# A loop that may run no times, put inside a conditional branch (one-core decoder trunk with a mixture of experts)

## The chip, the cores and the metric

The kernel runs on one core of a Trainium2 chip, as one launch. The metric is the device time in microseconds (us) of that launch. A measurement of a kernel is the median over several runs; beside it one execution is taken by the hardware profiler, and all rows below come from that one.

## The reference, cut to what matters

A decoder trunk of two layers on 512 tokens of width 1024. Each layer has a mixer (layer 0: a recurrent head group beside a gating group; layer 1: latent attention), a cross attention into 256 memory tokens, and a mixture of experts. The last is what matters here. Each token goes to the best of 4 groups and there to the best 2 of 8 experts, so 1024 assignments are spread over 32 experts:

```python
h = jax.nn.silu(xb @ w_gate[e]) * (xb @ w_up[e])      # 1024 -> 512
y = h @ w_down[e]                                     # 512 -> 1024
x <- LayerNorm(alpha * x + sum over the token's two experts of gate * y)
```

How many tokens an expert gets is known only at run time. The reference has room for any number.

## The kernel before, in words

**The expert stage** (`moe`, L1843) runs once per layer. It takes the 32 experts two at a time: 16 pairs, each with one tile of 128 rows, 64 for either expert (`CAP = 64`, two column groups of 64 on TensorE). Each pair is an `ExpertRows` object. `gather` (L1683) is an indirect DMA that GpSimd issues: it fetches the pair's 128 rows of h from DRAM into the one tile xg. `turn` (L1693, L1694) transposes them on TensorE (px) and copies them to xT on VectorE. `first` (L1704) does the gate projection into pg, or the up projection into pu, 32 matmuls of 128x512 each. `turn_hidden` (L1716, L1719) transposes the hidden rows hh by 4 matmuls (ph) and copies them back. `second` (L1730) is the down projection into py, 32 matmuls; ScalarE and VectorE split it into a high and a low part (L1736, L1737). `scatter` (L1677) builds a selection matrix on VectorE, and `combine` (L1744, L1754) adds the pair's rows to h by matmuls (pc) and VectorE adds.

**The weights** (`ExpertWeights`, L1494) come in pieces of 1 MB, 12 to a pair: 4 of the gate (wg), 4 of the up (wu), 4 of the down projection (wd). SyncE issues them in the order of use into a ring of buffers, as buffers come free (the `dma_start` is in the helper at L104). The last two pieces of a layer are issued as four halves (L1524). Before the loop below, `load_until_spare` issues what the ring can take, so that one buffer of the ring is left over for the loop; the four halves are asked for behind the loop.

**The extra blocks** (`overflow`, L1757). If an expert has more than 64 tokens, the rest is done in extra blocks of 128 rows. The function counts the blocks on VectorE (`nt`), loads the count into a register of every engine (`values_load`, L1793), and runs a loop of that many turns (`tc.For_i`, L1794). A turn finds its expert, fetches that expert's weights by indirect DMAs into the spare buffer, and does the whole row of gather to combine. The loop's bookkeeping (branches, semaphore events) has the line L1794.

**The order.** `overflow` is called in the turn of the second to last pair (`n == len(X) - 2`), after its gate and up projection and after all of the pair before has been combined. Behind it stand the gather for the last pair, the second to last pair's `turn_hidden`, `second` and `scatter`, and the last pair's `turn`. Then the last pair runs gate, up, combine of the pair before, down, and the layer norm follows. SyncE's and TensorE's order is the program's (`manual_schedule`); that of VectorE, ScalarE and GpSimd is set by the framework's planner, but nothing is moved across the loop. In layer 0 the key projection of the next layer's cross attention (`filler`: memory rows xr, weights wr, splits at L218 and L219, matmuls at L212) runs beside the layer norm.

Of the kernel before, what the change touches and what calls it, by code (L numbers as in the profile page):

```python
# [10 lines left out]
F32 = mybir.dt.float32  # L11
F32R = mybir.dt.float32r
BF16 = mybir.dt.bfloat16
I32 = mybir.dt.int32
AF = mybir.ActivationFunctionType
ALU = mybir.AluOpType
AX = mybir.AxisListType
# [3 lines left out]
P = 128  # L21
T = 512
NT = T // P
D = 1024
KD = D // P
NE = 32
FF = 512
FD = FF // P
# [1728 lines left out]
def overflow(k, pool, work, l, rt):  # L1757

    nc, tc, A, c = k.nc, k.tc, k.A, k.cst
    V = nc.vector  # L1760
    cap = CAP
    NB = 16

    def tl(shape, name, dt=F32):
        return pool.tile([P] + list(shape), dt, name="o" + name)

    cnt = rt["R"][:, NT]
    nb = tl([NE], "nb")
    V.tensor_scalar(nb, cnt, float(cap), None, op0=ALU.is_gt)
    for q in range(1, 4):  # L1770
        V.scalar_tensor_tensor(nb, cnt, float(cap + q * P), nb, op0=ALU.is_gt, op1=ALU.add)
    inc = tl([NE], "inc")
    V.tensor_tensor_scan(inc, c["one"][:, :NE], nb, 0.0, op0=ALU.mult, op1=ALU.add)
    base = tl([NE], "base")
    V.tensor_tensor(base, inc, nb, op=ALU.subtract)
    nt = tl([1], "nt", I32)
    V.tensor_copy(nt, inc[:, NE - 1:NE])

    R = rt["R"][:, :NT]
    t = tl([NT, NE], "t")  # L1780
    V.tensor_scalar(t, R, float(cap), -1.0e6, op0=ALU.is_lt, op1=ALU.mult)
    V.scalar_tensor_tensor(t, R, -float(cap), t, op0=ALU.add, op1=ALU.add)
    b128 = tl([NE], "b128")
    V.tensor_scalar(b128, base, 128.0, None, op0=ALU.mult)
    V.tensor_tensor(t, t, b128[:, None, :].to_broadcast([P, NT, NE]), op=ALU.add)
    key = tl([2, NT], "key")
    tm = tl([NT, NE], "tm")
    for j in range(2):
        V.tensor_tensor(tm, rt["o32"][j], t, op=ALU.mult)
        V.tensor_reduce(key[:, j], tm, axis=AX.X, op=ALU.add)  # L1790
    cur = tl([1], "cur")
    V.tensor_scalar(cur, base[:, 0:1], 0.0, None, op0=ALU.mult)
    n = nc.values_load(nt[0:1, 0:1], min_val=0, max_val=NB - 1)  # L1793
    with tc.For_i(0, n, 1):  # L1794
        c128 = tl([1], "c128")
        V.tensor_scalar(c128, cur, 128.0, None, op0=ALU.mult)
        koff = tl([2, NT], "koff")
        V.tensor_scalar(koff, key, c128, None, op0=ALU.subtract)

        le = tl([NE], "le")  # L1800
        V.tensor_scalar(le, inc, cur, None, op0=ALU.is_le)
        ex = tl([1], "ex")
        V.tensor_reduce(ex, le, axis=AX.X, op=ALU.add)
        V.tensor_scalar(ex, ex, float(l * NE), None, op0=ALU.add)
        wi = tl([2, KD], "wi")
        V.scalar_tensor_tensor(wi[:, 0], ex.to_broadcast([P, KD]), float(D), c["krow"], op0=ALU.mult, op1=ALU.add)
        V.scalar_tensor_tensor(wi[:, 1, :FD], ex.to_broadcast([P, FD]), float(FF), c["frow"], op0=ALU.mult, op1=ALU.add)
        V.tensor_copy(wi[:, 1, FD:], wi[:, 1, :KD - FD])
        wx = tl([2, KD], "wx", I32)
        V.tensor_copy(wx, wi)  # L1810

        po = k.psum("t", name="povt")
        m = 0
        for j in range(2):
            for i in range(NT):
                oh = pool.tile([P, P], F32, name="ooh", tag="ooh", bufs=2)
                V.tensor_scalar(oh, c["iota"], koff[:, j, i:i + 1], None, op0=ALU.is_equal)
                nc.tensor.matmul(po[:, :2], oh, rt["vals"][j][:, i, :], start=(m == 0), stop=(m == 7))
                m += 1
        tg = tl([2], "tg")  # L1820
        V.tensor_copy(tg, po[:, :2])
        ti = tl([1], "ti", I32)
        V.tensor_copy(ti, po[:, 0:1])

        def wts(j, what, half):
            nk, nf = (2, D) if what == "d" else (4, FF)
            v = k.same_tile("wo").rearrange("p (a b) -> p a b", a=nk)
            src = A[{"g": "moe_w_gate", "u": "moe_w_up", "d": "moe_w_down"}[what]]
            for kk in range(nk):
                col = half * nk + kk  # L1830
                nc.gpsimd.indirect_dma_start(
                    out=v[:, kk, :], out_offset=None, in_=src.rearrange("l e r f -> (l e r) f"),
                    in_offset=IndirectOffsetOnAxis(ap=wx[:, 1 if what == "d" else 0, col:col + 1], axis=0))
            return v

        x = ExpertRows(k, pool, work, lambda: tg, lambda: ti, wts, 1)

        x.hidden = lambda: x.xg[:, :FF]
        x.scatter(), x.gather(), x.turn(), x.first("g"), x.first("u"), x.turn_hidden(), x.second(), x.combine()
        V.tensor_scalar(cur, cur, 1.0, None, op0=ALU.add)  # L1840


def moe(k, rs, l, last, filler=None):  # L1843
# [3 lines left out]
    with ExitStack() as st:  # L1847
# [22 lines left out]
        with tc.manual_schedule(engines={mybir.EngineType.PE}):  # L1870
            for n, x in enumerate(X):
                more = n + 1 < len(X)
                x.first("g")
                x.first("u")

                if n:
                    X[n - 1].combine(0, "ccyy")
                if n == len(X) - 2:

                    X[n - 1].combine(2, "cccc")  # L1880
                    W.load_until_spare()
                    overflow(k, pool, work, l, rt)
                    X[n + 1].gather()
                    x.turn_hidden(), x.second(), x.scatter(), X[n + 1].turn()
                    continue
                x.turn_hidden()
                if n:
                    X[n - 1].combine(2, "cccc")
                if more:
                    X[n + 1].turn()  # L1890
                    if n + 3 < len(X):
                        X[n + 2].gather()
                    x.second()
                    x.scatter()
# [189 lines left out]
```

## Time and profile before

| | |
|---|---|
| median of the runs | 2052.22 us (2052.0 to 2052.83, 3 runs) |
| the profiled execution, its own time | 2047.49 us |
| its span, first to last instruction | 2045.7 us |
| mean granted TensorE clock | 0.945 |
| TensorE matmuls busy | 1795.2 us (88%) |
| VectorE, ScalarE, GpSimd busy | 959.0, 449.2, 273.9 us |
| moved by DMA | 522.41 MB |

How to read it: a busy time counts an engine's instructions, not its branches, semaphore events or the issuing of a DMA. The engines' sequencers have rows of their own, with a q behind the name (SPq is SyncE's); branches and events stand there. The expert stages are at about 560 to 1070 us (layer 0) and 1510 to 2046 us (layer 1).

### The profile page before, as it was taken

How to read it: one execution, taken by the hardware profiler on the slowest of the kernel's cores; microseconds unless marked ns; L12 is line 12 of the kernel's file. 1: busy time of each engine (PE TensorE's matmuls, PEld its weight loads, DVE VectorE, ACT ScalarE, POOL GpSimd, SP SyncE). 2: the span in 40 equal slices, each digit the busy share in tenths (PEclk: the TensorE clock that was granted, in tenths of full speed). 3: DMA queues.
4: the chain of work that ended last, by engine and by line, in shares of the span. 5: the costliest groups of instructions: out<-in, count | busy, mean ns of one | idle time of the engine just before them, and what ended most of it. 6: DMA issues, size and time to landing. Idle time of an engine off the chain costs nothing.

```text
span 2045.7 us, 23508 instructions
## 1 busy us (share of the span) xinstructions
PE 1795.2 (88%) x9206; PEld 1104.3 (54%) x9206; DVE 959.0 (47%) x2053; ACT 449.2 (22%) x834; POOL 273.9 (13%) x226
## 2 busy tenths in 40 slices
PE   8778989999789999898497999989969999988945
PEld 6567867878633444343136866778843444333312
DVE  5596466844723333233135666484552333233215
ACT  6314223343200000000022555343220000000000
POOL 3521532400200000000031000130010000000001
PEclk9887989999889999999798999999979999999968
DMA  5111106365789999999954200352869999999961
GB/s 189 54 62 43 31 21 218 122 207 182 301 347 420 421 419 420 421 421 421 400 175 166 83 21 21 103 176 72 340 243 418 421 421 421 420 420 421 421 270 62
DMA packets 124339, 522.41 MB, mean 255 GB/s; under 512 B 11937, under 2 KB 45889, under 8 KB 75585
## 3 DMA queue, kind: packets, MB, share of 16 engines
q1 hardware_dynamic: 114576, 486.58, 60.3%
q0 software_dynamic: 7056, 25.89, 3.6%
q10 hardware_dynamic: 2592, 8.40, 1.0%
q8 instruction: 74, 1.21, 0.2%
q14 instruction: 41, 0.33, 0.0%
HBM read 506.14 MB, written 14.69 MB: 255 GB/s over the span
## 4 chain that ended last, share of the span: by engine, by line
PE 54%; DMA 26%; DVE 13%; ACT 2%; issue 2%; POOL 2%; SPq 0%; DVEq 0%; ACTq 0%; POOLq 0%
DMA wu<-in_moe_w_up_dram 9%; DMA wd<-in_moe_w_down_dram 8%; DMA wg<-in_moe_w_gate_dram 7%; PE pu L1704 6%; PE py L1730 6%; PE pg L1704 6%; PE ptm L213 3%; PE pc L1744 3%; PE ptm L214 3%; PE ptm L212 3%; PE pcm L212 2%; PE pcm L213 2%; PE pcm L214 2%; PE po L1389 2%; PE psc L1356 2%
## 5 line engine op out<-in xcount | busy, mean ns | idle before, releaser
L1704 PE MATMUL pu<-wu,xT 128*64 128x512 f32 x1024 | 241.5, 595 | 28.0 <-DMA wu<-in_moe_w_up_dram 28.0
L1704 PE MATMUL pg<-wg,xT 128*64 128x512 f32 x1024 | 235.0, 598 | 1.0 <-DVE xT L1694 0.7
L1730 PE MATMUL py<-wd,hh 128*64 128x512 f32 x1024 | 232.2, 602 | 1.6 <-DVE hh L1719 1.6
L1710 DVE TENSOR_TENSOR hh<-hh,pu 128x512 f32<-128x512 f32 x32 | 22.0, 687 | 444.1 <-PE pu L1704 444.1
L1736 ACT ACTIVATE wy<-py,tab 128x512 fp32r<-128x512 f32 x64 | 43.8, 687 | 692.1 <-PE py L1730 675.7
L1704 PEld LDWEIGHTS pu<-wu,xT 128*64 128x64 f32 x1024 | 77.5, 137 | 183.3 <-issue 127.0
L1744 PE MATMUL pc<-wy,wc 128*128 128x512 f32 x480 | 139.2, 420 | 27.9 <-DVE h L1754 27.9
L1704 PEld LDWEIGHTS pg<-wg,xT 128*64 128x64 f32 x1024 | 80.0, 138 | 146.2 <-issue 133.0
L1754 DVE TENSOR_TENSOR h<-h,pc 128x512 f32<-128x512 f32 x240 | 151.1, 680 | 8.5 <-PE pc L1744 8.5
L1683 POOL DMA_INDIRECT xg<-rows,idx x32 | 30.2, 945 | 910.0 <-PE px L1693 716.6
L1730 PEld LDWEIGHTS py<-wd,hh 128*64 128x64 f32 x1024 | 71.8, 139 | 138.4 <-issue 132.4
L1744 PEld LDWEIGHTS pc<-wy,wc 128*128 128x128 f32 x480 | 81.5, 189 | 86.1 <-DVE h L1754 50.5
L1737 DVE SCALAR_TENSOR_TENSOR wy<-py,tab,wy 128x512 fp32r<-128x512 f32 x64 | 47.8, 750 | 170.5 <-ACT wy L1736 166.9
L212 PE MATMUL ptm<-wh,oh 128*128 128x512 f32 x192 | 75.7, 394 | 0.0
L219 DVE TENSOR_TENSOR wl<-wt,wh 128x1024 fp32r<-128x1024 f32 x37 | 48.1, 1306 | 58.2 <-ACT wh L218 57.6
L218 ACT CAST wh<-wt 128x1024 fp32r<-128x1024 f32 x50 | 51.7, 1049 | 106.9 <-PE ptm L214 61.2
L214 PE MATMUL ptm<-wh,ol 128*128 128x512 f32 x192 | 75.0, 391 | 0.0
L213 PE MATMUL ptm<-wl,oh 128*128 128x512 f32 x192 | 75.0, 391 | 0.0
L1716 PE MATMUL ph<-cst,hh 128*128 128x128 f32 x128 | 21.4, 292 | 56.3 <-issue 54.2
L1708 ACT ACTIVATE hh<-pg 128x512 f32<-128x512 f32 x32 | 19.1, 597 | 227.7 <-PE pg L1704 227.7
L212 PE MATMUL pcm<-xh,wh 128*128 128x512 f32 x144 | 61.4, 427 | 6.8 <-ACT xh L218 6.8
L214 PE MATMUL pcm<-xh,wl 128*128 128x512 f32 x144 | 60.5, 420 | 0.5 <-DVE wl L219 0.5
(532 smaller groups left out, 3396.7 us busy)
## 6 DMA issues: line engine op xcount, KB each, us to landing
wg<-in_moe_w_gate_dram SPq DMA_DIRECT2D x128, 1024.0 KB, 19.8
wu<-in_moe_w_up_dram SPq DMA_DIRECT2D x128, 1024.0 KB, 20.1
wd<-in_moe_w_down_dram SPq DMA_DIRECT2D x124, 1024.0 KB, 20.2
wr<-in_ab_w_in_dram SPq DMA_DIRECT2D x8, 1024.0 KB, 5.7
wr<-in_xa_wkv_dram SPq DMA_DIRECT2D x8, 1024.0 KB, 11.9
wt<-in_xa_wkv_dram SPq DMA_DIRECT2D x8, 1024.0 KB, 5.1
wr<-in_xa_wq_dram SPq DMA_DIRECT2D x8, 1024.0 KB, 6.3
wt<-in_xa_wo_dram SPq DMA_DIRECT2D x8, 1024.0 KB, 7.3
```

The costliest lines, as they stand in the source:

```text
L212: nc.tensor.matmul(out, lh, rh, start=start, stop=False)
L213: nc.tensor.matmul(out, lh, rl, start=False, stop=False)
L214: nc.tensor.matmul(out, ll, rh, start=False, stop=stop)
L218: k.nc.scalar.copy(hi, src)
L219: (eng or k.low()).tensor_tensor(lo, src, hi.bitcast(F32), op=ALU.subtract)
L1356: nc.tensor.matmul(ps[:, :n], qE[h][:, i * P:(i + 1) * P], kE[h % 2][(h // 2) % NB][:, :n], start=True, stop=False)
L1704: nc.tensor.matmul(ps[j * M:(j + 1) * M, :], self.xT[:, half * 4 + kk, j * M:(j + 1) * M], w[j][:, kk, :], start=(half == 0 and kk == 0), ...
L1730: nc.tensor.matmul(py[n][j * M:(j + 1) * M, :], self.hT[:, half * 2 + kk, j * M:(j + 1) * M], w[j][:, kk, n * 512:(n + 1) * 512], start=(h ...
L1736: nc.scalar.activation(yh, py[n], AF.Copy, scale=self.tab()[:, 1:2])
L1737: nc.vector.scalar_tensor_tensor(yl, py[n], self.tab()[:, 1:2], yh.bitcast(F32), op0=ALU.mult, op1=ALU.subtract)
L1744: self.k.nc.tensor.matmul(ps, self.C[:, i * P:(i + 1) * P], y, start=start and not last, stop=last)
L1754: k.nc.vector.tensor_add(k.h[:, i, s], k.h[:, i, s], pc)
```

## The change

The loop is put into a conditional block. Without the change of indentation the diff is one line:

```diff
     n = nc.values_load(nt[0:1, 0:1], min_val=0, max_val=NB - 1)
-    with tc.For_i(0, n, 1):
-        c128 = tl([1], "c128")
+    with tc.If(n > 0):
+        with tc.For_i(0, n, 1):
+            c128 = tl([1], "c128")
...
```

All of the loop's body goes one step further in, and nothing in it differs. `n` is the count of extra blocks, in a register of every engine. With a count of zero the loop's turns run in neither kernel.

## Rows read from the trace of the kernel before

**Rows 1.** The page: busy tenths in 40 slices, here TensorE and DMA.
```profile
PE   8778989999789999898497999989969999988945
...
DMA  5111106365789999999954200352869999999961
```

**Rows 2.** Chain that ended last, 900 to 1100: start, length (us), what.
```profile
1002.68 19.76 DMA wd<-in_moe_w_down_dram
1022.44 1.01 issue
```

**Rows 3.** Waits of TensorE, 995 to 1025, then 1944 to 1975: total, times, longest.
```profile
PE ph L1716 <- issue: 26.9, 1, 26.9
...
PE ph L1716 <- issue: 27.3, 1, 27.3
```

**Rows 4.** Waits of SyncE's queue, 995 to 1030, then 1945 to 1980.
```profile
SPq L1794 <- DMA wu<-in_moe_w_up_dram: 13.1, 1, 13.1
...
SPq L1794 <- DMA wd<-in_moe_w_down_dram: 4.8, 2, 2.4
...
SPq L1794 <- DMA wd<-in_moe_w_down_dram: 18.1, 1, 18.1
```

**Rows 5.** Line L1794 by stretches: ns least/median/most, first and last start.
```profile
L1794 ACTq COMPARE_BRANCH  x2: 38/44/50, 982.9 to 983.0; - x2
...
L1794 SPq COMPARE_BRANCH  x2: 38/46/53, 1004.0 to 1004.1; - x2
...
L1794 PEldq COMPARE_BRANCH  x3: 100/179/310, 996.5 to 1023.2; - x3
...
L1794 PEldq EVENT_SEMAPHORE  x1: 51/51/51, 1020.0 to 1020.0; - x1
```

**Rows 6.** Timeline around the loop, first stage: start, us, [idle before <-releaser].
```profile
996.03 1.29 DVE L1754 TENSOR_TENSOR h<-h,pc 128x512 f32<-128x512 f32 x2 [0.23 <-PE pc L1744]
...
1023.44 1.13 PE L1716 MATMUL ph<-cst,hh 128*128 128x128 f32 x4 [26.85 <-issue]
1023.90 0.94 POOL L1683 DMA_INDIRECT xg<-rows,idx  x1 [85.83 <-issue]
...
1034.24 1.16 PE L1693 MATMUL px<-cst,xg 128*128 128x128 f32 x8
```

**Rows 7.** Stretches: length, busy of PE, PEld, DVE, ACT, POOL; PEclk, DMA share, GB/s.
```profile
1004.00:1022.40 18.40, 0.00 (x0) 0.00 (x0) 0.00 (x0) 0.00 (x0) 0.00 (x0) 0.50 0.90 373
1022.40:1028.00 5.60, 3.77 (x12) 1.52 (x14) 1.56 (x5) 0.00 (x0) 0.94 (x1) 0.50 0.65 217
```

**Rows 8.** Timeline of the pair before, on TensorE.
```profile
963.52 0.63 PE L1716 MATMUL ph<-cst,hh 128*128 128x128 f32 x4
...
968.22 7.09 PE L1730 MATMUL py<-wd,hh 128*64 128x512 f32 x32
```

**Rows 9.** Timeline around the loop, second stage.
```profile
1945.37 1.29 DVE L1754 TENSOR_TENSOR h<-h,pc 128x512 f32<-128x512 f32 x2 [0.23 <-PE pc L1744]
...
1983.60 1.16 PE L1693 MATMUL px<-cst,xg 128*128 128x128 f32 x8
```

**Rows 10.** Gathers 900 to 960; weight loads at L104, 960 to 1060: issue and landing.
```profile
DMA to landing us min/median/max: 9.0/9.1/9.1
...
L104 SPq DMA_DIRECT2D wu<-in_moe_w_up_dram x8: 327/328/328, 960.5 to 997.7; - x8
L104 SPq DMA_DIRECT2D wd<-in_moe_w_down_dram x6: 328/328/328, 970.4 to 1002.7; - x6
...
DMA to landing us min/median/max: 11.6/19.8/19.8
```

**Rows 11.** Timeline behind the first stage: SyncE's next load, GpSimd's splits, TensorE's key projection.
```profile
1049.73 0.33 SPq L116 DMA_DIRECT2D xT<-in_ln_g_dram  x1
...
1063.92 9.45 POOL L219 TENSOR_TENSOR ws<-wr,ws 128x1024 fp32r<-128x1024 f32 x4
...
1076.85 0.52 PE L212 MATMUL pcm<-mh,ws 128*128 128x256 f32 x1 [3.64 <-DVE h L178]
```

More of the change, by code (lines that the diff above doesn't have):

```diff
@@ L1793, in overflow @@
     n = nc.values_load(nt[0:1, 0:1], min_val=0, max_val=NB - 1)
-    with tc.For_i(0, n, 1):
-        c128 = tl([1], "c128")
[L1796 to L1840, printed above, removed]
@@ new lines, in overflow, with wts @@
+    with tc.If(n > 0):
+        with tc.For_i(0, n, 1):
+            c128 = tl([1], "c128")
+            V.tensor_scalar(c128, cur, 128.0, None, op0=ALU.mult)
+            koff = tl([2, NT], "koff")
+            V.tensor_scalar(koff, key, c128, None, op0=ALU.subtract)
+            le = tl([NE], "le")
+            V.tensor_scalar(le, inc, cur, None, op0=ALU.is_le)
+            ex = tl([1], "ex")
+            V.tensor_reduce(ex, le, axis=AX.X, op=ALU.add)
+            V.tensor_scalar(ex, ex, float(l * NE), None, op0=ALU.add)
+            wi = tl([2, KD], "wi")
+            V.scalar_tensor_tensor(wi[:, 0], ex.to_broadcast([P, KD]), float(D), c["krow"], op0=ALU.mult, op1=ALU.add)
+            V.scalar_tensor_tensor(wi[:, 1, :FD], ex.to_broadcast([P, FD]), float(FF), c["frow"], op0=ALU.mult, op1=ALU.add)
+            V.tensor_copy(wi[:, 1, FD:], wi[:, 1, :KD - FD])
+            wx = tl([2, KD], "wx", I32)
+            V.tensor_copy(wx, wi)
+            po = k.psum("t", name="povt")
+            m = 0
+            for j in range(2):
+                for i in range(NT):
+                    oh = pool.tile([P, P], F32, name="ooh", tag="ooh", bufs=2)
+                    V.tensor_scalar(oh, c["iota"], koff[:, j, i:i + 1], None, op0=ALU.is_equal)
+                    nc.tensor.matmul(po[:, :2], oh, rt["vals"][j][:, i, :], start=(m == 0), stop=(m == 7))
+                    m += 1
+            tg = tl([2], "tg")
+            V.tensor_copy(tg, po[:, :2])
+            ti = tl([1], "ti", I32)
+            V.tensor_copy(ti, po[:, 0:1])
+            def wts(j, what, half):
+                nk, nf = (2, D) if what == "d" else (4, FF)
+                v = k.same_tile("wo").rearrange("p (a b) -> p a b", a=nk)
+                src = A[{"g": "moe_w_gate", "u": "moe_w_up", "d": "moe_w_down"}[what]]
+                for kk in range(nk):
+                    col = half * nk + kk
+                    nc.gpsimd.indirect_dma_start(
+                        out=v[:, kk, :], out_offset=None, in_=src.rearrange("l e r f -> (l e r) f"),
+                        in_offset=IndirectOffsetOnAxis(ap=wx[:, 1 if what == "d" else 0, col:col + 1], axis=0))
+                return v
+            x = ExpertRows(k, pool, work, lambda: tg, lambda: ti, wts, 1)
+            x.hidden = lambda: x.xg[:, :FF]
+            x.scatter(), x.gather(), x.turn(), x.first("g"), x.first("u"), x.turn_hidden(), x.second(), x.combine()
+            V.tensor_scalar(cur, cur, 1.0, None, op0=ALU.add)
```

## The prediction

> **What bounds the kernel now.** I read the slices of the page first, then the chain of waits around the one slice that stands out, then the waits themselves, and last the instructions of the loop's line. In the slices TensorE is at nine tenths through the expert stages, with two dips to four tenths (slice 20 of 40, and slice 39); in the first of them the DMA engines are as full as in the slices before it [rows 1]. The chain shows what the first dip is: a weight load wd issued at 1002.68 holds everything until 1022.44, then comes 1.01 us of "issue" [rows 2]. That load is for the last pair of experts, while the work that starts behind it, at 1023.44, is the hidden transposes (L1716) of the pair before, whose weights landed long ago. So no operand is late. The waits say the same: in front of L1716 TensorE stands 26.9 us in the first expert stage and 27.3 us in the second, put down to "issue", which is time for which the profile shows no producer [rows 3].
>
> The reason is on SyncE's queue. At L1794, the loop's own line, it waits 13.1 + 4.8 us for landings of wu and wd in the first stage and 18.1 us in the second [rows 4]. The rows of L1794 give the order. There are three branches per engine. ScalarE has done two by 983.0, SyncE two by 1004.1; TensorE's three run from 996.5 to 1023.2, and its semaphore event at 1020.0 lies between [rows 5]. No instruction of the loop's body is in the trace, so the count was zero in both layers. I read this as: branch over the body, count up, branch to the loop's end, and there every engine waits until every load under way has landed; then the third branch. Each engine makes the first two in its own time, without meeting the others. The stop is therefore paid behind the skip, at the loop's end, by a loop that runs no times. During its 18.4 us nothing computes and the DMA share is 0.90 [rows 7].
>
> **The change part by part.** It moves no computation. It puts one more test in front of the loop, and when the count is zero all of the loop goes, its end with the landings included, unless the new branch has such an end of its own.
>
> *Removed, first stage.* What has to be found is when the turn of the last pair's rows (px, L1693) starts, since from there all is one row on TensorE. It starts at 1034.24 now [rows 6]. In the changed kernel VectorE is the last engine to reach the branch that anything waits for: its last add starts at 996.03 and takes 1.29, end 997.32 [rows 6]. Add 0.4 for its branches and event: 997.7. Two chains start there. TensorE: transposes at the fast level, 0.63 (now 1.13), copy 0.69 and hand-over, together about 1.5, then the down projection, 7.09 as in the pair before [rows 6, 8]: 1006.3. GpSimd: the gather for the last pair, which stands behind the loop too, starts about 0.7 after the branch as it does now (1023.90 against TensorE's third branch at 1023.2) [rows 5, 6], so at 998.4, and needs 9.1 under full queues [rows 10]: 1007.5. The gather is late by 1.2, a wait that is hidden now because TensorE is slow. px starts at 1007.5 instead of 1034.24: 26.7 us. Bounds: with the quicker gather it is TensorE's 1006.3 (27.9 us); with 0.6 more on the gather 26.0.
>
> Of this some 2 us is TensorE's clock. In the stop the granted clock is 0.50, the lower of its two levels (1.2 GHz), and still 0.50 in the 5.6 us after it [rows 7]. With a gap of about one us left I take the fast level to hold. If it fell all the same, the gain shrinks to about 25.
>
> *Removed, second stage.* The same with its rows: VectorE's last add ends at 1945.37 + 1.29 = 1946.66, release 1947.1, gather 1947.8 to 1956.9, against px at 1983.60 [rows 9]: 26.7 us.
>
> *What is late next.* The weights of the last pair. The last wu is issued at 997.7, the last wd of the first half at 1002.7, landing 19.8 us later, at 1017.5 and 1022.5 [rows 10]. The gate projection starts about 1008.8 and has as many matmuls as the down projection, so 7.1; the up projection starts at 1015.9 and wants its last half 3.5 later, at 1019.4: landed. Four smaller wd loads stand on SyncE behind the loop; they are issued at about 1004.5 instead of 1023.0, 2.1 MB that at 373 GB/s [rows 7] take 5.6 and land by 1028.0. SyncE now issues the next loads when the up projection is done, 1049.73 [rows 11], so at 1023.0 then, into a queue with 5.0 us of work in it, where it is empty now. In the first stage these loads feed the key projection of the next layer: GpSimd's last split ends at 1063.92 + 9.45 = 1073.4, and TensorE takes it at 1076.85 after waiting 3.64 for VectorE, so 3.5 are covered [rows 11]. The loss lies between 0 and 5.0; I take 1.0, nearer to 5.0 less 3.5. The second stage has no such loads behind it.
>
> *Added.* One more test per engine: TensorE's branches take 0.10 to 0.31 [rows 5], and TensorE is free from 996.6, before VectorE, so it is covered up to about 1 us; on VectorE it is inside the 0.4. Below nothing it cannot be. In the other branch nothing runs.
>
> Sum: 26.7 + 26.7 - 1.0 = 52.4 us. The profiled execution took 2047.5 (span 2045.7), 4.7 less than the median of 2052.2; the stop is the same piece in either. 2047.5 - 52.4 = 1995.1 on that execution, 2052.2 - 52.4 = 1999.8 against the median. Forecast 2000.
>
> **Rivals.**
> *The stop stays.* A branch that joins again may need an end like the loop's, since the code behind it is the same whether the loop ran or not; then the landings are awaited there. For it: the loop does just that for a count of zero. Against it: within the loop's own skip the two first branches are made without a meeting, with only a short event between them [rows 5]. No gain, and up to 0.5 us of tests in each layer: 2052 to 2053.
>
> *A cheaper meeting, or a slow jump.* If the join makes the engines meet but not the loads, TensorE waits for SyncE, which comes last, at 1004.1, because it first has to place its loads [rows 5]; that is 6.4 later than 997.7 and leaves some 20 us per layer: 2052.2 - 39 = 2013. If the jump leads to code that has first to be brought in behind full queues, the price is not in the trace; the nearest row is the gather's 9.1 as the upper bound and the 0.31 of the skip that exists as the lower [rows 5, 10]; at the upper one: 2052.2 - 52.4 + 18.2 = 2018. Against the jump: the skip that exists is made by TensorE in 0.31 in the middle of a full queue.
> The Trainium skill (Runtime: NRT & Kernel Launch, section Instruction fetch mechanics) says that a taken branch whose target is outside the window of fetched pages stalls the engine while the page is brought in. By that rule this rival would hold in both layers; the 0.31 of the branch that already leaps the body does not bear it out, but the new leap is a little longer.
>
> *Slower.* The stop stays and the new jump behind it lands on code that is not there: place, the join; price, up to 9.1 per layer [rows 10], on TensorE's path because nothing else runs then. It decides against the kernel from 2.1 us per layer on. 2052.2 + 2 x (0.5 + 2.1 to 9.1) = 2057 to 2071.
>
> **How the numbers follow.** Forecast 0.76, its own range 1993 to 2008 (gain per layer 25 to 27.9, loss 0 to 5.0, and some us for another order of the work on the next phase's engines). Cheaper meeting or slow jump 0.08, 2008 to 2020. Stop stays 0.11. Slower 0.05. The range 1992 to 2022 leaves out the last two and little else. About 0.2%, 4 us, is what can be told from no change: faster 0.84, same 0.11, slower 0.05.
>
> **What would show it.** Right: on the rows of this line no event at the landing times; L1716 on TensorE within 2 us of the last combine matmul; granted clock 1.00 across; the gather within 2 us of VectorE's last add, landing about 9 us later, and px waiting up to 1.5 us for it; the four last wd loads issued straight behind the others; some us of wait for key weights in the next phase of the first layer. Wrong: a wait of over 5 us before L1716 in either layer, whoever it is put down to; or the 27 us coming back as waits for wu and wd in the last pair, which would say that the loads bound the end and not the stop.

## The result, and the profile after

The changed kernel took 1996.7 us (median of 4 runs, 1995.08 to 1997.93) against 2052.1 for the kernel before measured beside it (4 runs, 2047.94 to 2052.83): a ratio of 0.9734, 95% interval 0.9717 to 0.975. The forecast was 2000.0. The profiled execution took 1995.74 (span 1994.0), 51.75 less than the 2047.49 (span 2045.7) of before; worked out were 52.4 and 1995.1.

The page, TensorE and the DMA engines in 40 slices, now of 49.85 us each. Neither of the two dips to four tenths [rows 1] is left: slices 20 and 21, on either side of 997, show eight and nine tenths, slice 39 eight.

```profile
PE   8778998999969999989896999989969999989885
DMA  5210105464779999999995200243678999999993
```

The waits, 995 to 1030 and then 1895 to 1960: engine, tile and line, the releaser, total us, times, longest. In place of 26.9 and 27.3 us of "issue" in front of L1716 [rows 3] TensorE waits 1.1 and 0.9, for the event that VectorE sets behind its branch (DVEq is VectorE's own sequencer). Behind that the gather is waited for, 1.3 and 1.2 us.

```profile
PE px L1693 <- DMA xg<-rows,idx: 1.3, 1, 1.3
PE ph L1716 <- DVEq L1794: 1.1, 1, 1.1
...
PE px L1693 <- DMA xg<-rows,idx: 1.2, 1, 1.2
PE ph L1716 <- DVEq L1794: 0.9, 1, 0.9
```

The rows of L1794, which is now the branch's line, 930 to 1050: operation, count, ns least/median/most, first and last start. One branch is left on each engine, against three; the loop itself, now L1795, has no row at all, and no event stands at the landing of a weight load. One landing is still awaited at the branch: GpSimd, which reaches it 59 us ahead of TensorE, at 937.2, waits there from 937.3 to 946.1, when the gather that it had issued at 936.8 has landed (9.1 us to landing). No instruction is seen to wait for GpSimd then. TensorE's one branch takes 0.35 us and its event comes at 996.5, ahead of VectorE's at 997.1. SyncE reaches its branch at 1003.5, when TensorE has been at work behind it for six us.

```profile
L1794 POOLq EVENT_SEMAPHORE  x4: 17/43/43, 937.3 to 946.1; - x4
...
L1794 PEldq COMPARE_BRANCH  x1: 353/353/353, 996.1 to 996.1; - x1
L1794 PEldq EVENT_SEMAPHORE  x1: 51/51/51, 996.5 to 996.5; - x1
L1794 DVEq COMPARE_BRANCH  x1: 72/72/72, 996.9 to 996.9; - x1
L1794 DVEq EVENT_SEMAPHORE  x1: 21/21/21, 997.1 to 997.1; - x1
L1794 SPq COMPARE_BRANCH  x1: 50/50/50, 1003.5 to 1003.5; - x1
```

The timeline of the first stage: start, length, [idle before <-releaser]. The last add ends at 996.93, the gather is issued at 997.87 and px starts at 1007.21, where it started at 1034.24 [rows 6].

```profile
995.64 1.29 DVE L1754 TENSOR_TENSOR h<-h,pc 128x512 f32<-128x512 f32 x2 [0.23 <-PE pc L1744]
997.27 0.72 PE L1716 MATMUL ph<-cst,hh 128*128 128x128 f32 x4 [1.07 <-DVEq L1794]
997.87 0.94 POOL L1683 DMA_INDIRECT xg<-rows,idx  x1 [60.10 <-DVE wc L1677]
998.81 7.09 PE L1730 MATMUL py<-wd,hh 128*64 128x512 f32 x32 [0.82 <-DVE hh L1719]
1006.09 7.72 SPq L1524 DMA_DIRECT2D wd<-in_moe_w_down_dram  x4
1007.21 1.13 PE L1693 MATMUL px<-cst,xg 128*128 128x128 f32 x8 [1.31 <-DMA xg<-rows,idx]
...
1022.74 0.33 SPq L116 DMA_DIRECT2D xT<-in_ln_g_dram  x1
...
1033.26 2.79 ACT L218 CAST mh<-xr 128x256 fp32r<-128x256 f32 x8 [16.81 <-DMA xr<-in_memT_dram]
```

And of the second stage, where px started at 1983.60 and the last add ended at 1946.66 [rows 9]: 36.94 us between the two, now 1931.85 - 1921.82 = 10.03.

```profile
1920.53 1.29 DVE L1754 TENSOR_TENSOR h<-h,pc 128x512 f32<-128x512 f32 x2 [0.23 <-PE pc L1744]
...
1931.85 1.13 PE L1693 MATMUL px<-cst,xg 128*128 128x128 f32 x8 [1.20 <-DMA xg<-rows,idx]
```

What became of the gain on its way is read from one landmark in the phase between the stages, the first cast of a key tile on ScalarE (the row of that line: before, then after; first and last start):

```profile
L218 ACT CAST kTe<-pcm x8: 370/372/374, 1081.5 to 1105.0; 128x256 fp32r<-128x256 f32 x8
```
```profile
L218 ACT CAST kTe<-pcm x8: 372/372/374, 1056.2 to 1079.8; 128x256 fp32r<-128x256 f32 x8
```

At px the changed kernel is 27.0 us ahead (0.4 of it ahead of the stop already), at the key cast 25.3, at the last add of the second stage 1946.66 - 1921.82 = 24.8, and the second stage adds 26.9: 51.7, the difference of the spans.

### The profile page after: what moved, and what is told of

It reads as the page before. It is cut to its first block, busy times and chain, and to the rows that moved or that the text cites. A ratio compares the mean times of both kernels' runs of the same rounds, so it can differ in the third digit from the quotient of the medians.

```text
span 1994.0 us, 23447 instructions
## 1 busy us (share of the span) xinstructions
PE 1794.0 (90%) x9206; PEld 1106.6 (55%) x9206; DVE 958.7 (48%) x2053; ACT 448.9 (23%) x834; POOL 273.9 (14%) x226
## 5 line engine op out<-in xcount | busy, mean ns | idle before, releaser
L218 ACT CAST wh<-wt 128x1024 fp32r<-128x1024 f32 x50 | 51.7, 1049 | 107.5 <-PE ptm L214 61.8
L1708 ACT ACTIVATE hh<-pg 128x512 f32<-128x512 f32 x32 | 19.1, 597 | 229.5 <-PE pg L1704 229.5
L213 PE MATMUL pcm<-xl,wh 128*128 128x512 f32 x144 | 60.6, 421 | 0.1
```

The source lines that it names most:

```text
L213: nc.tensor.matmul(out, lh, rl, start=False, stop=False)
L218: k.nc.scalar.copy(hi, src)
```

## Experiments

The theory: the loop costs the wait for its landings at its end, with no iteration made; the skip takes that away in each layer, and no other part of the edit matters. Rivals: something beside the skip gives the time (the block itself, another place of the code); and, for what is left over, the gather or the order on ScalarE. The kernel before, measured beside each, had medians of 2049.34 (13 runs; one layer at a time, the branch always taken, the loop moved), 2048.91 (9; the four kernels told of last) and 2050.08 (7; fewer loads, the branch moved).

**One layer at a time.** Edits of the changed kernel:

```diff
-    with tc.If(n > 0):
+    with (tc.If(n > 0) if l == 0 else ExitStack()):   # the second run: l == 1
```

> The branch stands around the loop in layer 0 only; layer 1 keeps the bare loop. Theory (the cost is the wait for landings at the loop's end, once per layer, and the branch skips it): layer 0 gains what it gains in the changed kernel, 25.3 us as seen at the hidden transposes of the next phase, and layer 1 keeps its 27 us in front of L1716, so a span of about 2020.5 and some 2022 to 2027 at the median. Rival (the gain comes from another order of the work on the planner's engines that the new block brings about in the whole program): the two layers do not part cleanly, and the wait in front of L1716 in layer 1 is not the 27 us of before.

> The branch in layer 1 only. Theory: 26.9 us from layer 1, none from layer 0: a span of about 2019, 2020 to 2026 at the median, and the two single gains add up to that of the changed kernel within 2 us. Since the lower gain of layer 0 is put down to loads behind the stage that layer 1 does not have, e2 should gain 1.5 us more than e1. Rival (order of the work): the sum of the two is off by more than 3 us.

Branch in layer 0: 2024.00, ratio 0.9875 (0.9859 to 0.9892). Branch in layer 1: 2022.69, ratio 0.9869 (0.9853 to 0.9886). The gains, 25.3 and 26.7, add up to 52.0; the changed kernel measured again (below) has 51.6, so the two layers part cleanly. TensorE's waits of the first of them: 1.1 us where the branch is, the whole stop where it is not.

```profile
PE ph L1716 <- issue: 27.1, 1, 27.1
...
PE ph L1716 <- DVEq L1794: 1.1, 1, 1.1
```

Layer 0 gives 1.3 us less at the medians, where 1.5 was expected; that fits the loss behind it.

**A branch that is always taken.** The block stays, the loop inside it is reached.

```diff
-    with tc.If(n > 0):
+    with tc.If(n < 15):
```

> The test is n < 15, true for a count of zero: the branch is there, and its inside, the loop that runs no times, is entered. Theory: the stop is back in both layers, 26 to 28 us in front of L1716, 2045.7 to 2047.5 in span; what the branch adds on top is under 0.5 us per layer. Rival (the block as a wall alone changes the order and so the time): the time lies near that of the changed kernel, 1994 to 2000.

2049.57, ratio 0.9998 (0.9989 to 1.0008; 10 runs). The block alone gives and costs nothing that can be measured. (The span of 2045.7 to 2047.5 was missed by the profiled execution, 2051.8, which was the slowest of the ten.) In its waits both stops are back, and SyncE's queue stands at the loop's line, now L1795, for 13.0 and 4.8 us in the first stage as before [rows 4]:

```profile
PE ph L1716 <- issue: 54.2, 2, 27.2
```
```profile
SPq L1795 <- DMA wu<-in_moe_w_up_dram: 13.0, 1, 13.0
...
SPq L1795 <- DMA wd<-in_moe_w_down_dram: 4.8, 2, 2.4
```

**The loop of before, moved to where fewer loads matter.** No branch; the call stands behind the last pair's gate and up projections.

```diff
                     W.load_until_spare()
-                    overflow(k, pool, work, l, rt)
                     X[n + 1].gather()
 ...
+        with tc.manual_schedule(engines={mybir.EngineType.PE}):
+            overflow(k, pool, work, l, rt)
         sums = {}
```

> No branch: the kernel of before, with the bare loop moved behind the last pair's gate and up projection and the combining of the pair before. Theory (the loop's end waits for what is under way): at that place, about 1026, the last load of the queue has landed at 1022.5, so the stop shrinks to 1 to 3 us per layer; the four last wd loads are now asked for behind the loop, land 6 to 8 us after it, and may cost 0 to 4 us before the down projection; span 1996 to 2008. Rival (the loop as such costs 27 us, by its branches, the meeting of the engines, or the leap over its code): 2045 wherever the loop stands.

2010.42 (2009.13 to 2013.59), ratio 0.9811 (0.9793 to 0.9829): 2 us beyond the upper end that was expected, but most of the stop is gone without any branch. SyncE's queue still waits at the loop's line for the landings as long as before, and then another 5.1 us for VectorE, which gets there later (L1793 is its load of the count). TensorE, which works until it gets there, waits 2.2 us. The waits in 995 to 1030 on SyncE, then those of TensorE in 1020 to 1050:

```profile
SPq L1794 <- DMA wu<-in_moe_w_up_dram: 13.1, 1, 13.1
...
SPq L1794 <- DVEq L1793: 5.1, 1, 5.1
SPq L1794 <- DMA wd<-in_moe_w_down_dram: 4.8, 2, 2.4
```
```profile
PE pacc L1902 <- issue: 2.2, 1, 2.2
PE pc L1744 <- DVE h L1754: 1.0, 1, 1.0
PE py L1730 <- DMA wd<-in_moe_w_down_dram: 0.2, 1, 0.2
```

So the long part of the loop's end is a wait for loads under way, which costs only an engine that arrives before they have landed. Two things remain. TensorE reaches the loop at 1031.2, 4.5 us after the last of these loads has landed (1026.7), and its 2.2 us go by with the loop's branches and events. And the loop's end is a meeting as well: SyncE stands there until VectorE has come, so the loads behind the loop go out late. Those of the next phase (xr) are issued at 1036.5, 12.9 us later than in the changed kernel, and the first key cast comes at 1069.6, 13.4 later, of a difference of 15.9 between the two spans. The granted clock behind the 2.2 us was 0.74 to 0.79 for the next 7.6, which is part of the rest.

**Fewer loads under way at the loop.** In the kernel before, `load_until_spare` now takes 11 pieces instead of 15. The 15th is one of the two that are asked for later as halves and gets only its buffer, so three loads fewer are issued ahead of the loop, the last wu and two wd; SyncE issues them at 1016.7 to 1017.5, behind it.

```diff
-        for _ in range(max(j for j in used if rings[j][2] == 1)):
+        for _ in range([j for j in used if rings[j][2] == 1][-5]):
```

> No branch: the kernel of before, in which SyncE issues 11 loads ahead of the loop instead of all 15 that the ring has room for. The last wu and the first wd of the last pair are then not under way when the loop is reached. Theory (the loop's end waits for the last landing): the last load under way is the third wu, landing at 1015.1 instead of 1022.5, one piece of 1 MB being 2.45 us; the wait in front of L1716 falls from 26.9 to about 19.5 in both layers, and the time by 14 to 15 us, to about 2034. Rival (the stop has a length of its own): 27 us and 2049 as before.

2034.56 (2032.17 to 2037.84), ratio 0.993 (0.9913 to 0.9946). TensorE waits until the last load then under way has landed, 19.5 us in layer 0, as expected, and 19.1 in layer 1, and this time the profile names the load. Its waits in 995 to 1030:

```profile
PE ph L1716 <- DMA wu<-in_moe_w_up_dram: 19.5, 1, 19.5
```

With the row of the loop moved this settles the cause: the length of the stop is set by the loads, but for one to two us of the loop's own (1.01 behind the last landing [rows 2], 2.2 where the loads had landed).

**The branch moved in the same way.** The edit of the moved loop, made in the changed kernel.

> The changed kernel with the branch moved behind the last pair's gate and up projection, as the bare loop was in e4. Theory: no gap of TensorE in front of L1716, px 7.7 us after VectorE's last add instead of 10 to 11.8; but the four last wd loads are asked for about 20 us later and may hold up the down projection by 0 to 3 us; in layer 0 the loads of the next phase take back what is won. 1993 to 1998. Rival (the place is indifferent once the branch skips the stop): within 1 us of 1997.

2004.83 (2001.9 to 2007.49), ratio 0.9782 (0.9766 to 0.9798): a miss. The gain over the kernel before, measured beside it, is 45.3 us instead of the 51.6 of the changed kernel measured again. The reason is on SyncE's queue (its waits, then its timeline):

```profile
SPq L1524 <- PEq L1794: 19.7, 1, 19.7
```
```profile
1008.24 24.70 SPq L1524 DMA_DIRECT2D wd<-in_moe_w_down_dram  x4
```

The last pair's wd loads stand behind the branch, and one of them waits until TensorE has passed it, at about 1030. Here a late branch on TensorE holds back SyncE's next loads, those of the next phase included: xr is issued at 1034.0 instead of 1023.6, and the first key cast comes at 1066.5 instead of 1056.2, 10.3 us later. From the last add of the second stage on, which has no such loads behind it, the two kernels take the same time (72.1 and 72.2 us).

**What is left of the cost.** Four kernels, beside one another: the changed kernel again; without loop and branch; the last pair's gather ahead of the branch; and the last pair's second half given priority in the planner's order.

```diff
-    n = nc.values_load(nt[0:1, 0:1], min_val=0, max_val=NB - 1)
-    with tc.If(n > 0):                # and all of the loop: "no loop"
 ...
-                    overflow(k, pool, work, l, rt)
                     X[n + 1].gather()
+                    overflow(k, pool, work, l, rt, X[n + 1])     # "early gather"
 ...
+        with tc.high_priority():      # "priority"
         x.second()
```

> The changed kernel once more, on the chip of the three that follow, as their yardstick. 1995 to 1998 at the median, L1716 behind the branch after 0.9 to 1.1 us of wait, px after 1.2 to 1.3 us of wait for the gather.

> The load of the count, the branch and the loop are left out (full experts' extra blocks would not be computed; there are none in these inputs). It shows what the branch that is skipped still costs. Theory: 1.0 us in front of L1716 and 1.2 us in front of px in each layer, because the gather can now go before the second to last pair is done; in layer 0 part of it is lost again to the loads behind. 3 to 5 us less than the changed kernel. Rival (a skipped branch is free, px would wait for something else): within 1 us of the changed kernel.

> The gather for the last pair is issued ahead of the branch; the loop's blocks use the same tile, and the branch fetches the rows again at its end. Theory: the 1.2 us of wait in front of px goes in both layers, the 1.0 us in front of L1716 stays: 1.5 to 2.5 us less than the changed kernel. Rival (the gather's landing stands beside something else that is as late, such as the high and low split of py): 0 to 1 us less.

> In the changed kernel the last pair's down projection, with its split on ScalarE and VectorE, is given the planner's high priority. Theory: the 1.8 us that layer 0 gains less than layer 1 is ScalarE's order, two casts of key weights in front of the split of py while their loads are late; with the split first, the accumulators of layer 0 run on as in the kernel of before, and 1 to 1.8 us are won, in layer 0 alone. Rival (the loads themselves are the limit, GpSimd's and VectorE's splits of the key weights end as late): the split comes earlier and the next phase starts no earlier, within 0.5 us.

Measured: 1997.33 for the changed kernel (0.9743, 0.973 to 0.9756), 2000.03 without loop (0.9758, 0.9745 to 0.9772), 1996.74 with the early gather (0.9744, 0.973 to 0.9758), 1997.31 with priority (0.9744, 0.973 to 0.9759). The early gather and priority cannot be told from the changed kernel. Without the loop it is slower: each of the five runs (1998.59 to 2002.73) lies above each of the changed kernel's five (1994.5 to 1998.2). All three improvements that I had expected are misses, and so is the wait for the gather in the changed kernel's second profile; the early gather and priority came out by the numbers of their rivals.

In the profile of the early gather the gather would not have come last. The down projection in front of px took 8.71 us there (8.78 in layer 1), and 9.74 in the changed kernel's second profile, whose px waited for no gather at all; what the early gather gives where the projection takes 7.09 no run shows (timelines: the changed kernel again, then early gather):

```profile
997.19 0.95 PE L1716 MATMUL ph<-cst,hh 128*128 128x128 f32 x4 [1.06 <-DVEq L1794]
...
998.93 9.74 PE L1730 MATMUL py<-wd,hh 128*64 128x512 f32 x32 [0.78 <-DVE hh L1719]
...
1008.60 1.16 PE L1693 MATMUL px<-cst,xg 128*128 128x128 f32 x8
```
```profile
1002.81 8.71 PE L1730 MATMUL py<-wd,hh 128*64 128x512 f32 x32 [0.82 <-DVE hh L1719]
```

That is the clock. In the same stretch after the same gap it was 1.00 in the first profile of the changed kernel and 0.50 in the second (first fence and second; columns as in [rows 7]):

```profile
999.00:1003.00 4.00, 4.00 (x20) 1.30 (x19) 0.00 (x0) 0.00 (x0) 0.00 (x0) 1.00 1.01 414
```
```profile
999.00:1003.00 4.00, 4.00 (x10) 1.17 (x12) 0.00 (x0) 0.00 (x0) 0.00 (x0) 0.50 1.00 409
```

Without the loop TensorE has no gap, and px stands 7.7 us behind the last add in either layer, 2.4 to 2.6 earlier than in the first profile of the changed kernel. In layer 0 that does not arrive: the first key cast comes 60.7 us after the last add, against 59.2 and 59.7 in the two profiles of the changed kernel. ScalarE's casts of the next phase's stripe (mh) stand there in another order, behind a result of the last down projection, and so start at 1042.9 instead of 1033.3; in the changed kernel they wait for the load alone:

```profile
1042.30 0.69 ACT L1736 ACTIVATE wy<-py,tab 128x512 fp32r<-128x512 f32 x1 [22.35 <-PE py L1730]
1042.88 0.40 ACT L218 CAST mh<-xr 128x256 fp32r<-128x256 f32 x1
```

Why the kernel without loop is 2.7 us above the changed one at the medians is not settled beyond that. Its profiled execution, the slowest of its five, starts its very first px 3.7 us later than the changed kernel's second (572.9 against 569.2), ahead of what the edit touches. With priority the first key cast came 60.5 us after the last add, and mh still waited for its load (17.4 us): at that cast the load is the limit in both orders.

## Why the prediction was right, point by point

*The loop's end waits for landings, with no iteration made.* Right, and shown: the stop shrinks with the loads (19.5 us with three fewer), stays with a branch that does not skip (27.2), and goes with one that does. That each engine does this waiting itself shows in the kernel before: on L1794 each of the five has an event at 1017.6, at 1020.0 and at 1022.5, when the last wu and the two wd land. What the prediction did not have is that the engines also meet there, which the moved loop shows (5.1 us on SyncE).

*Removed, 26.7 us in each layer.* Measured from the last add to px: 36.92 less 10.28 in layer 0, 36.94 less 10.03 in layer 1, so 26.6 and 26.9. The step that set px, the gather at 1007.5, was 1007.0 and px 1007.21. TensorE's own chain was as worked out too, 1005.9 against 1006.3, since the down projection took 7.09. (The lower bound, with 0.6 more on the gather, adds up to 26.1 and not to 26.0.)

*The clock holds over a gap of one us.* Right in the first profile of the changed kernel and not in general: the second profile of the same program has 9.74 in layer 0 and 9.99 in layer 1 instead of 7.09. Of the ten places in the profiles where a skipped branch stands in front of L1716, the projection behind it took 7.09 in three. That the first profile had it in both layers was luck, and so is a part of the close fit of the sum to it. From the last add to px the second profile took 11.74 and 11.66 us instead of 10.28 and 10.03: 1.5 and 1.6 per layer and not the 2.6 to 2.9 of the projection, since the gather's wait of 1.2 to 1.3 is used up by it. This is the prediction's "shrinks to about 25", worked out there as 1.7 less per layer.

*The loss of 1.0 between the stages, bounds 0 to 5.0.* About 1.7 at the key cast, 2.2 with what follows up to the second stage. The direction was right and the path was not. I had GpSimd's splits of the key weights in mind, with 3.5 us of slack. What is late is ScalarE's first cast of the loaded stripe (mh from xr), for which it waits 16.8 us. From SyncE's first load of that phase (L116) to that cast it now takes 1033.26 - 1022.74 = 10.5 us; before it took 1057.91 - 1049.73 [rows 11] = 8.2, by this row of the kernel before:

```profile
1057.91 1.32 ACT L218 CAST mh<-xr 128x256 fp32r<-128x256 f32 x4 [14.42 <-DMA xr<-in_memT_dram]
```

The four last wd loads were issued from 1006.1 to 1013.8, not at 1004.5, since SyncE waits at them for earlier loads to land (8.4 us in all). They still landed at 1028.5, near the 1028.0 worked out, so the next phase's loads, from 1022.74 on, found 5.8 us of work ahead of them (5.0 in the sum). That it is these four wd loads and no others that delay xr was not tried by itself.

*The added test is covered.* Right: 0.35 us on TensorE from 996.1, ahead of VectorE's event at 997.1. The wait for VectorE's branch was in the sum at 0.4 us and measures 0.34 from the last add's end to L1716. Not in it was that without loop and branch the transposes start 0.9 us ahead of that end; in the changed kernel, where the clock holds, the gather lands later than the projection ends in any case.

*The rivals.* "The stop stays" is out by the waits; what the branch keeps of such an end is GpSimd's wait for its own gather, which ends 50 us before TensorE's branch. "A cheaper meeting" holds for VectorE, at one us, and not for SyncE, whose branch at 1003.5 no one waits for. "A slow jump" is out: the branch over the whole loop takes 0.35 us on TensorE while the DMA engines are full (428 GB/s from 995.0 to 997.2), against 0.31 for the leap that existed.
The Trainium skill (Runtime: NRT & Kernel Launch, section Instruction fetch mechanics) has a taken branch out of the fetched pages stall its engine; this trace has no such stall on TensorE, whose event at 996.5 stands right behind its branch of 353 ns. Whether the target lay in a fetched page no row shows.

*The forecast against the median.* It was 3.3 us too high against the median of 1996.7, and 0.64 too low on the profiled execution (1995.1 against 1995.74). There the gain is accounted for: 27.0 at px, less 2.2 between the stages, and 26.9 in the second, against 52.4 in the sum. The 3.3 comes from the median of 2052.2 that the sum was taken off: it lies 4.7 above the profiled execution of the kernel before, while the changed kernel's median lies 1.0 above its own. The kernel before has medians of 2048.9 to 2050.1 in the later comparisons, and the gain was 51.6 there, not the 55.4 of the first.

## What to carry to other kernels

A dynamic loop that is there for a rare case is not free when its count is zero. In this kernel every engine waited at its end for every load then under way, so its price was read from what stood in the DMA queues at the loop: 27 us here, in a stage that prefetches far ahead, and 19.5 with three loads fewer. A test around the whole loop took this away. So, for the most part, did moving the loop to where the loads had landed before the engine that matters came; that cost about 2 us of the loop's own and held back the loads behind it. A branch that is skipped has a small meeting as well (0.9 to 1.1 us here); before moving it, look at which loads stand behind it on the issuing queue, since here they waited for the slower engine to pass.

## What was not expected of the hardware

Two executions of one program, with the same gap on TensorE (1.07 and 1.06 us), had a granted clock of 1.00 in the one and 0.50 in the other over the stretch from 999.0 to 1003.0, so that the same 32 matmuls took 7.09 and 9.74 us. Of the other kernels with this gap the projection took 9.89 with the branch in layer 0 alone, 9.59 with it in layer 1 alone, 8.71 and 8.78 with the early gather, and 8.78 and 7.09 with priority. One profile of such a place is not enough to say that the clock holds. And the loop's wait, put down to "issue" with nothing named in the kernel before, was put down to the right load where three loads fewer were ahead: "issue" in front of a long idle stretch can be a landing too.
